# Tiles of split operands made 32 bytes longer

## The chip, the core and the metric

The kernel runs on one core of a Trainium2 chip. The metric is the time of one execution on the device in microseconds (us). Of the kernel before there are three timed runs, 637.49 to 638.16 us with a median of 637.85, and one profiled execution, from which every duration below is taken.

The core's engines work at the same time and wait for each other by semaphores. PE (TensorE) multiplies matrices: a weight load (LDWEIGHTS, shown as PEld) puts the stationary operand into the array, then a matmul streams the moving operand through it. ACT (ScalarE) and DVE (VectorE) work element by element, POOL (GpSimd) does little here, and SP issues DMAs. Tiles lie in the on-chip memory as 128 partitions by so many bytes.

## The reference

A decoder trunk of two layers on 256 positions of width 1024, in float32. Each layer adds a token mixer and then a squared-ReLU channel mixer to the residual `h`, each on a normed input:

```
for i in range(2):
    u = rmsnorm(h, norm_mix[i])
    h = h + (dsw_mixer if i == 0 else moba_mixer)(u, w_qkv, q_gain, k_gain, w_o, rel_bias)
    h = h + square(relu(rmsnorm(h, norm_ffn[i]) @ w1)) @ w2          # 1024 -> 4096 -> 1024
```

The first mixer ("a") is dilated sliding-window attention: 24 heads of 64 in three groups of window and dilation, merged by their softmax denominators. The second ("b") is block-sparse attention with 16 heads; its block has 256 positions, so at this length it is causal attention. Both norm q and k per head and add a relative-position bias. All weights together are some 110 MB, and each is used once.

## The kernel before, in words

**Split operands.** The large products are computed from split float32 numbers. A weight `w` (after its gain) and an activation `u` each become a high part, rounded to the type float32r, and a low part, the rest. `mm3` (L228 to L231) then adds three matmuls in one accumulator in PSUM: high by high (L229), high by low, low by high. The product of the low parts is left out. In the up-projection of the channel mixer the three are written out (L652 to L654).

**The weight stream.** All weights are cut into units of 256 rows by 512 columns, in the order of use (`plan`). SP loads a unit into one of 5 `raw` tiles. ACT makes the high part (`next_hi`, L165 without and L167 with a gain) and DVE the low part (`next_lo`, L175 and L177). They are written into one of 7 `hi` and one of 7 `lo` tiles, each of 128 partitions by 2 by 512 numbers, 4096 bytes a partition. `weight` hands a slice of 128 rows to the matmuls, and `used` gives a unit back. `beat`, called every one or two groups of matmuls, paces the stream: on every second beat it makes one more slice, and it starts whatever was put off by `defer` to this beat. So the order on each engine is written out by the program; no planner reorders it.

**The activations.** `norm_transpose` turns a half of the residual by PE into PSUM, and ACT and DVE split it into the pair `u` (two halves of 4 by 256 numbers, high and low, one buffer each: 4 tiles). `project` multiplies u (stationary, 128 columns) by the weights (moving, 512 columns) for q, k and v. `attend` computes logits, softmax and weighted values with plain float32 matmuls, and its `finish` splits the result into a pair of tiles of the tag `ol`, 4 buffers. `wo_group` multiplies these by the output weights (512 moving columns).

**The channel mixer.** In `ffn`, `up(j)` makes 512 of the 4096 hidden columns: here the weights are stationary (128 columns) and u is moving (256 columns). ReLU, square and split go to a pair `hh`, `hl` of the same tag `ol`. `down(j)` multiplies the pair (stationary) by the second weights (moving, 512 columns) into the accumulators `y`. `up(j + 1)` is issued ahead of `down(j)`, eight times, in each of two layers.

**Where tiles lie.** Pools follow each other in the memory, and the slots of a tag lie one after the other. The tiles that the change touches have a size of 4096 bytes each, a multiple of 128, and start at multiples of 128.

Of the kernel before, what the change touches and what calls it, by code (L numbers as in the profile page):

```python
# [25 lines left out]
F32R = mybir.dt.float32r  # L26
# [4 lines left out]
P = 128  # L31
S = 256
# [15 lines left out]
SPLIT = 7  # L48
# [19 lines left out]
def trunk(ctx, tc, x, rel_bias, norm_mix, norm_ffn, a_w_qkv, a_q_gain, a_k_gain, a_w_o,  # L68
# [4 lines left out]
    wp = ctx.enter_context(tc.tile_pool(name="wp", bufs=1))  # L73
    act = ctx.enter_context(tc.tile_pool(name="act", bufs=1))
# [6 lines left out]
    def bank(tag, name):  # L81
        return ps.tile([P, 512], F32, tag=tag, bufs=2, name=name)

    def work(tag, bufs, name):
        return act.tile([P, 512], F32, tag=tag, bufs=bufs, name=name)

# [43 lines left out]
    raw, split = {}, {}  # L130
# [21 lines left out]
    def parts(s):  # L152
        i, c = divmod(s, 2)
        return raw[i][:, c, :], split[i][0][:, c, :], split[i][1][:, c, :], units[i][1]

    def next_hi():
        i, c = divmod(st["hi"], 2)
        if i >= len(units) or i >= st["first"] + SPLIT:
            return False
        if c == 0:  # L160
            split[i] = (wp.tile([P, 2, 512], F32R, tag="hi", bufs=SPLIT, name=f"hi_{i}"),
                        wp.tile([P, 2, 512], F32R, tag="lo", bufs=SPLIT, name=f"lo_{i}"))
        w, hi, _, gain = parts(st["hi"])
        if gain is None:
            nc.scalar.activation(hi, w, AF.Copy)  # L165
        else:
            nc.scalar.activation(hi, w, AF.Copy, scale=gt[:, gain + c:gain + c + 1])  # L167
        st["hi"] += 1
        return True
# [19 lines left out]
    def weight(key, k):  # L189

        i = index[key, k // 2]
        s = 2 * i + k % 2
        st["asked"] = max(st["asked"], s + 1)
        while st["hi"] <= s:
            assert next_hi(), (key, k)
        while st["lo"] <= s:
            next_lo()
        return split[i][0][:, k % 2, :], split[i][1][:, k % 2, :]

    def used(key, k):  # L200
        done.add(index[key, k // 2])
        while st["first"] in done:
            st["first"] += 1

    def defer(beats, fn):
        st["seq"] += 1
        later.append((st["beat"] + beats, st["seq"], fn))

    def beat(n=1):

        for _ in range(n):
            st["beat"] += 1
            while True:
                due = sorted(e for e in later if e[0] <= st["beat"])
                if not due:
                    break
                later.remove(due[0])
                due[0][2]()
            if st["beat"] % 2 == 0 or st["lo"] < st["asked"] + 4:
                next_slice()  # L220
# [7 lines left out]
    def mm3(acc, a, b, first, last):  # L228
        nc.tensor.matmul(acc, lhsT=a[0], rhs=b[0], start=first, stop=False)  # L229
        nc.tensor.matmul(acc, lhsT=a[0], rhs=b[1], start=False, stop=False)  # L230
        nc.tensor.matmul(acc, lhsT=a[1], rhs=b[0], start=False, stop=last)  # L231


    h = const.tile([P, NT, D], F32, name="h")
# [15 lines left out]
    rel = lead.tile([REL_BUCKETS, NG * HG], F32, name="rel")  # L250
    nc.sync.dma_start(rel, rel_bias)
    idle = work("z", 3, "idle")[:, 0:P]
    nc.vector.memset(idle, 0.0)
    warm_ps = bank("o", "warm_ps")
# [87 lines left out]
    u = {}  # L342
    rstd = {}

    def norm_transpose(which, half, t, natural):

        if t == 0:
            u[half] = tuple(act.tile([P, 4, S], F32R, tag=f"u{half}{s}", bufs=1, name=f"u{s}_{which}_{half}")
                            for s in ("h", "l"))
        tp = bank("tp", f"ut_{which}_{half}_{t}")  # L350
        for c in range(4):
            k = 4 * half + c
            nc.tensor.transpose(out=tp[:, c * P:(c + 1) * P], in_=h[:, t, k * P:(k + 1) * P], identity=ident)
        hi, lo = u[half]
        i = tp.rearrange("p (c q) -> p c q", c=4)
        if natural:
            hi, lo = (z.rearrange("p c (q t) -> p t c q", t=NT)[:, t] for z in (hi, lo))
        else:
            hi, lo = (z[:, :, t * P:(t + 1) * P] for z in (hi, lo))
        nc.scalar.activation(hi, i, AF.Copy)  # L360
        nc.vector.tensor_sub(lo, i, hi.bitcast(F32))
# [40 lines left out]
    def ux(k, cols):  # L402
        hi, lo = u[k // 4]
        return hi[:, k % 4, cols], lo[:, k % 4, cols]


    V, T, oT = {}, {}, {}
# [79 lines left out]
    def attend(layer):  # L487
# [6 lines left out]
        bias, probs, turned, o = {}, {}, {}, {}  # L494
# [90 lines left out]
        def finish(p):  # L585

            if p % 4 == 0:
                oT[p // 4] = tuple(act.tile([P, 4, S], F32R, tag="ol", bufs=4, name=f"o{s}_{layer}_{p}") for s in "hl")
            hi, lo = (z[:, p % 4, :] for z in oT[p // 4])
            i = o[p][:, 0:S]  # L590
            if layer == "b":
                hi, lo = (z.rearrange("p (b t q) -> p t q b", b=2, t=2) for z in (hi, lo))
                i = i.rearrange("p (t q b) -> p t q b", t=2, b=2)
            nc.scalar.activation(hi, i, AF.Copy)
            nc.vector.tensor_sub(lo, i, hi.bitcast(F32))
# [28 lines left out]
    def ffn(i, after):  # L624
        hid, y = {}, {}

        def up(j):
            key = ("up", i, j)
            hh, hl = hid[j] = tuple(act.tile([P, 4, S], F32R, tag="ol", bufs=4, name=f"h{s}_{i}_{j}") for s in "hl")
            first = j == 0  # L630
            banks = {}

            def relu2(b, c0, n):
                w = n * S
                r = work("z", 3, f"r_{i}_{j}_{b}")[:, :w]
                defer(1, lambda: nc.scalar.activation(r, banks[b][:, :w], AF.Relu))  # L636
                ho, lo = (z[:, c0:c0 + n, :].rearrange("p c q -> p (c q)") for z in (hh, hl))
                defer(3, lambda: nc.vector.tensor_mul(r, r, r))  # L638
                defer(5, lambda: nc.scalar.activation(ho, r, AF.Copy))
                defer(7, lambda: nc.vector.tensor_sub(lo, r, ho.bitcast(F32)))  # L640

            for c, ks in [(c, r) for r in (range(4), range(4, 8)) for c in range(4)] if first else \
                    [(c, range(8)) for c in range(4)]:
                b, off = (c, 0) if first else (c // 2, c % 2 * S)
                if b not in banks:
                    banks[b] = bank("acc" if b < 2 else "o", f"up_{i}_{j}_{b}")
                o = banks[b][:, off:off + S]
                for k in ks:
                    whi, wlo = weight(key, k)
                    uh, ul = ux(k, slice(0, S))  # L650
                    cols = slice(c * P, (c + 1) * P)
                    nc.tensor.matmul(o, lhsT=whi[:, cols], rhs=uh, start=k == 0, stop=False)  # L652
                    nc.tensor.matmul(o, lhsT=whi[:, cols], rhs=ul, start=False, stop=False)  # L653
                    nc.tensor.matmul(o, lhsT=wlo[:, cols], rhs=uh, start=False, stop=k == 7)  # L654
                    if c == 3 and k % 2:
                        used(key, k)
                    if k % 2:
                        beat()
                if ks[-1] == 7 and first:
                    relu2(b, c, 1)  # L660
                elif ks[-1] == 7 and c % 2:
                    relu2(b, c - 1, 2)

        def down(j):
            hh, hl = hid[j]
            for n in range(2):
                key = ("down", i, j, n)
                if j == 0:
                    y[n] = [bank("so"[n], f"y_{i}_{n}_{t}") for t in range(NT)]
                tail = i == 1 and j == 7 and n == 1  # L670
                for k, t in [(k, t) for t in range(NT) for k in range(4)] if tail else \
                        [(k, t) for k in range(4) for t in range(NT)]:
                        q = slice(t * P, (t + 1) * P)
                        mm3(y[n][t], (hh[:, k, q], hl[:, k, q]), weight(key, k), j == 0 and k == 0, j == 7 and k == 3)
                        if t == 1 and k % 2:
                            used(key, k)
                        beat()
                if j == 7:
                    after(n, y[n])

        up(0)
        for j in range(8):
            if j < 7:
                up(j + 1)
            down(j)
# [105 lines left out]
```

## Time and profile before

| | |
|---|---|
| median of 3 runs | 637.85 us (637.49 to 638.16) |
| profiled execution | 637.99 us |
| its span, first to last instruction | 636.2 us |
| PE busy | 630.7 us, 3902 matmuls |
| PEld busy | 545.1 us, 3902 weight loads |
| DVE busy | 426.5 us |
| ACT busy | 384.3 us |
| POOL busy | 36.6 us |
| mean granted clock of PE | 0.999 of full speed |
| HBM read | 111.81 MB, 178 GB/s over the span |

The busy time of an engine is the time in which at least one of its instructions ran. Matmuls follow each other before the one ahead has ended, so a busy PE can still be faster or slower, and the distance between the starts of two matmuls says more than the duration of one. Arrows in the rows read "written <- read".

### The profile page before, as it was taken

The numbers are of one execution on the slowest core, as the hardware profiler recorded it, in microseconds if no ns is written. First come the engines' busy times: TensorE is split into PE (matmuls) and PEld (weight loads), VectorE is DVE, ScalarE is ACT, GpSimd is POOL, SyncE is SP. The second block draws the span as 40 slices with busy tenths as digits, with TensorE's granted clock in tenths as the row PEclk, the third lists the DMA queues.
The fourth block names the chain that finished last, engine by engine and source line by source line (L and its number), as shares of the span: only waits on it lengthen the run. The fifth ranks groups of instructions, "written<-read, shape, count | busy, mean of one in ns | idle before, by whom it ended". The sixth has DMA issues, their size and how long they took to land.

```text
span 636.2 us, 10379 instructions
## 1 busy us (share of the span) xinstructions
PE 630.7 (99%) x3902; PEld 545.1 (86%) x3902; DVE 426.5 (67%) x767; ACT 384.3 (60%) x742; POOL 36.6 (6%) x23
## 2 busy tenths in 40 slices
PE   8999999999999999999999999999999999999997
PEld 7778888778989989988988887777998899899886
DVE  5878989846865476467447789886776745754651
ACT  6876876665765365356437868766655644653540
POOL 1222230000000000000000322000000000000000
PEclk9999999999999999999999999999999999999999
DMA  7986566434655674574456566653467446645701
GB/s 247 318 197 229 130 199 173 144 100 123 213 162 185 214 223 132 179 261 137 167 179 201 198 187 188 165 164 122 152 199 261 134 170 229 208 132 192 250 15 67
DMA packets 74538, 113.62 MB, mean 179 GB/s; under 512 B 4584, under 2 KB 30504, under 8 KB 74488
## 3 DMA queue, kind: packets, MB, share of 16 engines
q1 hardware_dynamic: 74312, 112.82, 55.9%
q8 instruction: 31, 0.51, 0.3%
q14 instruction: 19, 0.16, 0.1%
q10 hardware_dynamic: 176, 0.14, 0.1%
HBM read 111.81 MB, written 1.13 MB: 178 GB/s over the span
## 4 chain that ended last, share of the span: by engine, by line
PE 98%; DMA 1%; DVE 0%; SPq 0%; DVEq 0%; issue 0%
PE up L654 10%; PE up L653 10%; PE up L652 10%; PE y L230 9%; PE y L231 9%; PE y L229 9%; PE acc_a L229 6%; PE acc_a L230 5%; PE acc_a L231 5%; PE acc_b L229 4%; PE acc_b L231 3%; PE acc_b L230 3%; PE s_a L518 1%; PE o_a L583 1%; PE wo_b L229 1%; PE wo_b L231 1%
## 5 line engine op out<-in xcount | busy, mean ns | idle before, releaser
L177 DVE SCALAR_TENSOR_TENSOR lo<-raw,gt,hi 128x512 fp32r<-128x512 f32 x248 | 174.7, 746 | 7.2 <-ACT hi L167 7.1
L167 ACT ACTIVATE hi<-raw,gt 128x512 fp32r<-128x512 f32 x248 | 162.9, 712 | 5.7 <-PE y L231 2.8
L652 PE MATMUL up<-uh,hi 128*128 128x256 f32 x512 | 145.1, 283 | 0.0
L654 PE MATMUL up<-uh,lo 128*128 128x256 f32 x512 | 144.9, 283 | 0.0
L653 PE MATMUL up<-ul,hi 128*128 128x256 f32 x512 | 144.9, 283 | 0.0
L175 DVE TENSOR_TENSOR lo<-raw,hi 128x512 fp32r<-128x512 f32 x152 | 98.7, 687 | 44.4 <-ACT hi L165 44.0
L165 ACT ACTIVATE hi<-raw 128x512 fp32r<-128x512 f32 x152 | 88.0, 623 | 54.1 <-PE y L231 28.1
L229 PE MATMUL y<-hi,hh 128*128 128x512 f32 x256 | 99.9, 390 | 0.0
L230 PE MATMUL y<-lo,hh 128*128 128x512 f32 x256 | 99.8, 390 | 0.0
L231 PE MATMUL y<-hi,hl 128*128 128x512 f32 x256 | 99.6, 389 | 0.0
L653 PEld LDWEIGHTS up<-ul,hi 128*128 128x128 f32 x512 | 98.2, 192 | 0.6
L652 PEld LDWEIGHTS up<-uh,hi 128*128 128x128 f32 x512 | 98.2, 192 | 0.5
L654 PEld LDWEIGHTS up<-uh,lo 128*128 128x128 f32 x512 | 98.2, 192 | 0.0
L638 DVE TENSOR_TENSOR r<-r 128x512 f32<-128x512 f32 (+1 forms) x36 | 22.7, 632 | 68.4 <-ACT r L636 68.4
L636 ACT ACTIVATE r<-up 128x512 f32<-128x512 f32 (+1 forms) x36 | 19.8, 550 | 76.1 <-PE up L654 75.7
L229 PE MATMUL acc_a<-hi,uh 128*128 128x512 f32 x144 | 60.6, 421 | 0.0
L230 PE MATMUL acc_a<-lo,uh 128*128 128x512 f32 x144 | 56.8, 395 | 0.0
L231 PE MATMUL acc_a<-hi,ul 128*128 128x512 f32 x144 | 56.8, 394 | 0.0
L231 PEld LDWEIGHTS y<-hi,hl 128*128 128x128 f32 x256 | 48.1, 188 | 10.0
L229 PEld LDWEIGHTS y<-hi,hh 128*128 128x128 f32 x256 | 48.1, 188 | 9.6
L230 PEld LDWEIGHTS y<-lo,hh 128*128 128x128 f32 x256 | 48.1, 188 | 9.5
L229 PE MATMUL acc_b<-hi,uh 128*128 128x512 f32 x96 | 40.2, 419 | 0.0
(128 smaller groups left out, 778.3 us busy)
## 6 DMA issues: line engine op xcount, KB each, us to landing
raw<-in_ffn_w_dram SPq DMA_DIRECT2D x128, 512.0 KB, 4.8
raw<-in_a_w_qkv_dram SPq DMA_DIRECT2D x64, 256.0 KB, 4.2
raw<-in_b_w_qkv_dram SPq DMA_DIRECT2D x24, 512.0 KB, 4.6
raw<-in_b_w_o_dram SPq DMA_DIRECT2D x8, 512.0 KB, 4.8
bias_a<-vdram_a SPq DMA_DIRECT2D x20, 128.0 KB, 5.9
raw<-in_a_w_qkv_dram SPq DMA_DIRECT2D x4, 512.0 KB, 6.5
raw<-in_a_w_o_dram SPq DMA_DIRECT2D x4, 512.0 KB
bias_b<-vdram_b SPq DMA_DIRECT2D x8, 256.0 KB, 4.9
```

Of the source, the lines that this page charges most:

```text
L165: nc.scalar.activation(hi, w, AF.Copy)
L167: nc.scalar.activation(hi, w, AF.Copy, scale=gt[:, gain + c:gain + c + 1])
L175: nc.vector.tensor_sub(lo, w, hi.bitcast(F32))
L177: nc.vector.scalar_tensor_tensor(lo, w, gt[:, gain + c:gain + c + 1], hi.bitcast(F32), op0=ALU.mult, op1=ALU.subtract)
L229: nc.tensor.matmul(acc, lhsT=a[0], rhs=b[0], start=first, stop=False)
L230: nc.tensor.matmul(acc, lhsT=a[0], rhs=b[1], start=False, stop=False)
L231: nc.tensor.matmul(acc, lhsT=a[1], rhs=b[0], start=False, stop=last)
L636: defer(1, lambda: nc.scalar.activation(r, banks[b][:, :w], AF.Relu))
L638: defer(3, lambda: nc.vector.tensor_mul(r, r, r))
L652: nc.tensor.matmul(o, lhsT=whi[:, cols], rhs=uh, start=k == 0, stop=False)
L653: nc.tensor.matmul(o, lhsT=whi[:, cols], rhs=ul, start=False, stop=False)
L654: nc.tensor.matmul(o, lhsT=wlo[:, cols], rhs=uh, start=False, stop=k == 7)
```

## The change

The helper `wide` allocates a tile of 1032 float32r numbers, 4128 bytes a partition, and returns a view on the first 1024 of them in the shape that was asked for. It takes the place of the plain allocation in four places: the tiles `hi` and `lo` of the split weights, the pairs `u`, and the two uses of the tag `ol` (attention output and hidden activations). The last 8 numbers of each tile are never written or read. No instruction's shape or order is edited. The tiles behind those in the memory move by multiples of 32 bytes.

```diff
+    def wide(pool, tag, bufs, name, a):
+
+        z = pool.tile([P, 1032], F32R, tag=tag, bufs=bufs, name=name)
+        return z[:, :1024].rearrange("p (a n) -> p a n", a=a)
...
         if c == 0:
-            split[i] = (wp.tile([P, 2, 512], F32R, tag="hi", bufs=SPLIT, name=f"hi_{i}"),
-                        wp.tile([P, 2, 512], F32R, tag="lo", bufs=SPLIT, name=f"lo_{i}"))
+            split[i] = tuple(wide(wp, part, SPLIT, f"{part}_{i}", 2) for part in ("hi", "lo"))
...
         if t == 0:
-            u[half] = tuple(act.tile([P, 4, S], F32R, tag=f"u{half}{s}", bufs=1, name=f"u{s}_{which}_{half}")
-                            for s in ("h", "l"))
+            u[half] = tuple(wide(act, f"u{half}{s}", 1, f"u{s}_{which}_{half}", 4) for s in "hl")
...
             if p % 4 == 0:
-                oT[p // 4] = tuple(act.tile([P, 4, S], F32R, tag="ol", bufs=4, name=f"o{s}_{layer}_{p}") for s in "hl")
+                oT[p // 4] = tuple(wide(act, "ol", 4, f"o{s}_{layer}_{p}", 4) for s in "hl")
...
-            hh, hl = hid[j] = tuple(act.tile([P, 4, S], F32R, tag="ol", bufs=4, name=f"h{s}_{i}_{j}") for s in "hl")
+            hh, hl = hid[j] = tuple(wide(act, "ol", 4, f"h{s}_{i}_{j}", 4) for s in "hl")
```

## Rows read from the trace of the kernel before

**Rows 1.** The page, busy us (share of the span) and instructions by engine.

```profile
PE 630.7 (99%) x3902; PEld 545.1 (86%) x3902; DVE 426.5 (67%) x767; ACT 384.3 (60%) x742; POOL 36.6 (6%) x23
```

**Rows 2.** The page, the chain of waits that ended last, by engine.

```profile
PE 98%; DMA 1%; DVE 0%; SPq 0%; DVEq 0%; issue 0%
```

**Rows 3.** Groups by line: xcount | busy us, mean ns | idle before; one of three each.

```profile
L652 PE MATMUL up<-uh,hi 128*128 128x256 f32 x512 | 145.1, 283 | 0.0
...
L229 PE MATMUL y<-hi,hh 128*128 128x512 f32 x256 | 99.9, 390 | 0.0
...
L229 PE MATMUL acc_a<-hi,uh 128*128 128x512 f32 x144 | 60.6, 421 | 0.0
...
L229 PE MATMUL acc_b<-hi,uh 128*128 128x512 f32 x96 | 40.2, 419 | 0.0
...
L229 PE MATMUL wo_b<-hi,oh_b 128*128 128x512 f32 x32 | 13.5, 423 | 0.0
...
L229 PE MATMUL wo_a<-hi,oh_a 128*128 128x512 f32 x16 | 7.0, 435 | 0.0
```

**Rows 4.** Timeline of PE, an up stretch: start us, us; first and 27th row.

```profile
235.81 0.28 PE L654 MATMUL up<-uh,lo 128*128 128x256 f32 x1
...
238.93 0.28 PE L653 MATMUL up<-ul,hi 128*128 128x256 f32 x1
```

**Rows 5.** Timeline of PE, a settled down stretch: first and seventh row.

```profile
300.08 0.39 PE L229 MATMUL y<-hi,hh 128*128 128x512 f32 x1
...
301.44 0.39 PE L229 MATMUL y<-hi,hh 128*128 128x512 f32 x1
```

**Rows 6.** Timeline of PE, the first projection: first, fourth, fifth and ninth of nine rows.

```profile
9.15 0.63 PE L231 MATMUL acc_a<-hi,ul 128*128 128x512 f32 x1
...
10.43 0.42 PE L231 MATMUL acc_a<-hi,ul 128*128 128x512 f32 x1
10.69 0.39 PE L229 MATMUL acc_a<-hi,uh 128*128 128x512 f32 x1
...
11.62 0.39 PE L230 MATMUL acc_a<-lo,uh 128*128 128x512 f32 x1
```

**Rows 7.** Timeline of PE, down after up: first and sixth matmul after the switch.

```profile
246.37 0.40 PE L229 MATMUL y<-hi,hh 128*128 128x512 f32 x1
...
247.53 0.39 PE L231 MATMUL y<-hi,hl 128*128 128x512 f32 x1
```

**Rows 8.** Timeline of PEld, the load for the second of these matmuls.

```profile
246.38 0.19 PEld L230 LDWEIGHTS y<-lo,hh 128*128 128x128 f32 x1
```

**Rows 9.** Timeline of PE, projection between logits: first and eighth of eight rows.

```profile
60.16 0.40 PE L231 MATMUL acc_a<-hi,ul 128*128 128x512 f32 x1
...
61.78 0.39 PE L229 MATMUL acc_a<-hi,uh 128*128 128x512 f32 x1
```

**Rows 10.** Groups by line, the splitting of weights on DVE and ACT.

```profile
L177 DVE SCALAR_TENSOR_TENSOR lo<-raw,gt,hi 128x512 fp32r<-128x512 f32 x248 | 174.7, 746 | 7.2 <-ACT hi L167 7.1
L167 ACT ACTIVATE hi<-raw,gt 128x512 fp32r<-128x512 f32 x248 | 162.9, 712 | 5.7 <-PE y L231 2.8 <-DMA raw<-in_a_w_qkv_dram 2.7 <-ACT hi L165 0.2
...
L175 DVE TENSOR_TENSOR lo<-raw,hi 128x512 fp32r<-128x512 f32 x152 | 98.7, 687 | 44.4 <-ACT hi L165 44.0
```

**Rows 11.** Windows: us, busy us (x) of PE, PEld, DVE, ACT, POOL, PEclk, DMA, GB/s.

```profile
330.00:400.00 70.00, 70.00 (x371) 57.02 (x370) 58.27 (x120) 53.64 (x117) 14.21 (x5) 1.00 0.62 188
...
6.00:18.00 12.00, 11.70 (x49) 9.31 (x50) 9.41 (x14) 10.11 (x20) 0.00 (x0) 1.00 0.91 309
```

**Rows 12.** Groups by line, weight loads before which PE waited for a lo.

```profile
L230 PEld LDWEIGHTS acc_a<-lo,uh 128*128 128x128 f32 x144 | 27.4, 190 | 4.8 <-DVE lo L177 0.5
```

**Rows 13.** Groups by line, the splitting of u.

```profile
L361 DVE TENSOR_TENSOR ul<-ut,uh 128x512 fp32r<-128x512 f32 x16 | 11.0, 690 | 10.5 <-ACT uh L360 10.4
...
L360 ACT ACTIVATE uh<-ut 128x512 fp32r<-128x512 f32 x16 | 9.6, 603 | 22.6 <-PE ut L353 22.6
```

**Rows 14.** The chain in order of time, its longest pieces: the first.

```profile
1.19 4.97 DMA h<-in_x_dram
```

## The prediction

> **What bounds the kernel now.** I read the busy times first. TensorE (PE) is busy for 630.7 of the 636.2 us [rows 1]. The chain of waits comes next, and it shows that this is no accident of the average: 98% of the chain that ended last is PE, and of the other engines only a DMA reaches 1% [rows 2]. So the time is the sum of the distances from one matmul's start to the next, and whatever is not in that sum has to be larger than its cover before it counts.
>
> The groups by line give the number of matmuls [rows 3]; the reader takes the counts there, and not the busy times, since those overlap (283 ns for a matmul that follows its neighbour after 120). Up-projection (three lines of 512) has 1536 matmuls with 256 moving columns. The others with split operands have 512 moving columns and come three lines each: y 768, acc_a 432, acc_b 288, wo_b 96, wo_a 48, together 1632. Every one of these 3168 reads a stationary and a moving operand from tiles that the change touches.
>
> The timeline gives the distance. In an up stretch the first row and the 27th start 3.12 us apart: 3.12 / 26 = 120.0 ns [rows 4]. In a settled down stretch six distances take 1.36 us: 226.7 ns [rows 5]. At 2.4 columns per ns, 256 and 512 columns are 106.7 and 213.3 ns, so that each of the matmuls has 13.3 ns over its columns, the same at both lengths. At the start the four rows show something else [rows 6]: three distances from 9.15 to 10.43 us, 427 ns each, which is 512 columns at 1.2 GHz, the lower of the clock's two levels, with nothing over (the clock's row on the page shows no lower level there; the distances do); from 10.69 us on four distances average 232 ns.
>
> The sum: 1536 x 120.0 = 184.3 us and 1632 x 226.7 = 370.0 us, 554.3 of the span of 636.2. The remaining 81.9 us are transposes, logits, the small matmuls, what lies around them and the two ends. What the change can reach on PE is the 13.3 ns: 3168 x 13.3 ns = 42.1 us.
>
> **The change part by part.** It adds no instruction, removes none, and moves none: every activation, subtraction, matmul and DMA has the same shape and order. It makes 22 slots longer by 32 bytes a partition (14 of hi and lo, 4 of u, 4 of the tag ol), 704 bytes together. Before, each of these tiles is 4096 bytes, a multiple of 128; after, 4128, so that the start of a slot moves through 0, 32, 64 and 96 modulo 128. A 128-column slice is 512 bytes and keeps its tile's offset. Three costs can follow.
>
> *PE's two reads.* While one matmul's moving operand streams, the next matmul's weights are loaded. In the trace the load starts at 246.38 us, with the matmul that started at 246.37 [rows 7, 8]. If both reads used one of four 32-byte places in turn and blocked each other where they met, 13.3 ns would be the price, and other offsets would change it. The bounds of that: of four offsets three differ from before, so up to 3/4 x 42.1 = 31.6 us could go (606.4 us from the profiled 637.99), and as much could come if the offset of today is the good one (669.6 us). The value I take is 0, for two reasons. First, the offset is not held: in up stretches one load of 128 columns (512 bytes) goes with 256 moving columns (1024 bytes), so the moving read runs 512 bytes, four times 128, ahead of the load in each matmul; in 512-column matmuls it is 1536 bytes, twelve times 128. At steady rates the two reads meet at each offset equally often wherever they start, and a shift of the start by 32 bytes changes which meeting is first, not how many there are. Secondly, 13.3 ns is the same for two lengths and for pairs of quite different tiles, which fits a fixed price of a weight change better.
>
> What speaks for a sensitivity is that the 512-column distance is not always 226.7. After a switch from up to y five distances average 232 ns [rows 7], and in the projection between transposes seven average 231.4 [rows 9]. They come at the same places of the pattern and settle, so they follow the spacing of loads and matmuls; a read that is sensitive to that by a few ns may be sensitive to 32 bytes too. The nearest row to a cost is therefore 5 ns on a 512-column matmul, 1632 x 5.0 = 8.2 us at most.
>
> The Trainium skill bears on this place ("TensorE: Matmul & The Clock Gate", section "Part 2: What happens when you issue a matmul"): it says that PE reads the moving operand and the weights through two independent ports, and that a load takes nothing from the running matmul. By that rule the padding is worth 0. The same page (section "Wait — 56ns, not 53.3ns?") has a matmul cost its columns plus about 2.5 ns at full clock; by an estimate from it, 3168 matmuls would lie 34 us lower than the rows show. The trace's 13.3 ns disagrees with the second statement, and this is why I don't hold the first for settled: by rule 637.9 us, by the row's remainder, were three quarters of it contention, about 612 us.
>
> *ScalarE and VectorE.* ACT writes hi, DVE reads raw and hi and writes lo; raw stays at 0 modulo 128, hi and lo shift. The costliest are 248 subtractions at 746 ns and 248 activations at 712 ns [rows 10]. I take 0. The bounds are from the rows: DVE's two-input forms lie between 687 and 746 ns, so I allow 59 ns either way for 400 subtractions, 23.6 us of DVE work. All of it lies beside PE: in the tightest long stretch DVE is busy 58.3 of 70 us and has 11.7 left, while about 70/636 of 23.6 us, 2.6 us, would be added [rows 11]. A gain there is worth nothing, as PE has waited for a lo only once, 0.5 us [rows 12]. Only at the start is there little cover: from 6 to 18 us ACT is busy 10.1 of 12 us. With 10% more there, up to 1 us would show.
>
> *Order and DMAs.* The tile is now one row of 1032 with a view on it. If dependencies were drawn more coarsely for the view, the place is u: its two writers per half each take every other 128 columns of four chunks, so that ranges of the two interleave. That would be a wait of ACT for DVE's 16 subtractions of 690 ns [rows 13], 11.0 us if all of them stood in PE's way, and 0 as I take it, since both halves of a tile are written before the matmuls that need them. Tiles behind the padded ones (z, q and k turned, bias, h) also move by multiples of 32 bytes. Of these h and bias are written by DMA; landings are slack except x at the start, where the chain has 4.97 us of it [rows 14]; a tenth of that either way is 0.5 us.
>
> Sum: 0 + 0 + 0. The profiled execution took 637.99 us (its span of 636.2 and 1.8 around it); the median of the three runs is 637.85, 0.14 lower. I forecast 637.8 us, no change. What counts as one is 0.2%, 1.3 us: about what a measurement of this kernel can tell.
>
> **The rivals.** *Faster: the reads of PE collide less.* For it: 13.3 ns at the full pace and nothing over at half the pace [rows 4 to 6] is how two reads that compete for one memory would look. Against it: the sweep through all offsets, and the equal price at both lengths. If one pair in four falls on a better offset, 42.1 / 4 = 10.5 us go: 627.3 us. *Slower: the settled rhythm is lost.* Its place is the 512-column matmuls, above all y, which now settle at 226.7. Where a pair's offset differs from before (three in four of 1632), the distance stays at the 231.7 ns of the unsettled stretches: 1224 x 5.0 = 6.1 us, 644.0 us. It decides as soon as the distance depends on more than about 1.3 us / 1632 = 0.8 ns per matmul. For it: rows 7 and 9; against it: unsettled distances follow a switch of shape or a transpose, and the addresses don't change there. *Slower: new waits for u.* 11.0 us exposed at most; half of it gives 643.4 us. Against it: same-engine writers need no wait. *The padding does nothing*, since slots are rounded up and stay 128 apart: 637.85 us, not to be told from my forecast by time, but by distances equal in every stretch.
>
> **How the numbers follow.** No change 0.58 (of this 0.03 that slots don't shift); faster by PE's reads 0.25; slower by a lost rhythm 0.12, by waits 0.05. Of the faster case I give 0.16 to sizes up to 10.5 us and 0.09 beyond; of the slower ones 0.13 up to 7 us and 0.04 beyond. A range from 627 to 645 us holds 0.58 + 0.16 + 0.13 = 0.87; drawn in further, it would end at prices that have a row behind them, and it stays open to 0.13 at the two ends of the bounds (606 and 670). The likeliest case's own range is 636.6 to 639.1.
>
> **What would show it.** Right: up distances of 120.0 ns and settled y distances of 226.7 ns in all stretches, whichever slots are in use, PE about 630.7 us busy, and chain as before; DVE's 746 and ACT's 712 ns within 10 ns. If PE's reads matter, distances differ from slot to slot in a cycle of the seven hi and lo slots, and the up stretches tell it at once, as 0.1 ns of all 1536 would be 0.15 us. Wrong in the DVE step: longer subtractions and PE idle before a lo. Wrong in the order step: idle of PE before the first matmuls after a norm. The forecast falls if the up or the y distance moves by more than 0.8 ns on average.

## The result, and the profile after

The changed kernel takes 641.61 us (median of 4 runs, 641.47 to 642.05), the kernel before, in 4 runs beside it, 637.87 (637.49 to 638.16). The ratio is 1.0060, 95% interval 1.0044 to 1.0076: slower by 3.7 us, or 0.6%. The forecast was no change.

The page of the changed kernel, busy times and the chain by engine, answers to [rows 1, 2]:

```profile
PE 633.6 (99%) x3902; PEld 542.8 (85%) x3902; DVE 426.4 (67%) x767; ACT 384.7 (60%) x742; POOL 36.6 (6%) x23
...
PE 98%; DMA 1%; DVE 0%; SPq 0%; ACT 0%; DVEq 0%; issue 0%; ACTq 0%
```

PE is still the whole chain, with as many instructions, and is busy 2.9 us longer; the span grew from 636.2 to 640.3 us. The other engines did not change. The costliest groups by line of the changed kernel, beside [rows 10, 13]:

```profile
L181 DVE SCALAR_TENSOR_TENSOR lo<-raw,gt,hi 128x512 fp32r<-128x512 f32 x248 | 174.6, 745 | 7.5 <-ACT hi L171 7.3
L171 ACT ACTIVATE hi<-raw,gt 128x512 fp32r<-128x512 f32 x248 | 163.0, 713 | 5.8 <-DMA raw<-in_a_w_qkv_dram 2.6
L179 DVE TENSOR_TENSOR lo<-raw,hi 128x512 fp32r<-128x512 f32 x152 | 98.6, 686 | 46.6 <-ACT hi L169 46.3
...
L364 DVE TENSOR_TENSOR ul<-ut,uh 128x512 fp32r<-128x512 f32 x16 | 11.0, 690 | 11.0 <-ACT uh L363 11.0
```

Each duration is within 1 ns of before. So the time lies in the distances between matmuls, and the timeline shows it. PE in the changed kernel, a stretch of y and the stretch of up behind it, first and last row of each:

```profile
230.43 0.40 PE L233 MATMUL y<-hi,hh 128*128 128x512 f32 x1
...
235.30 0.40 PE L233 MATMUL y<-hi,hh 128*128 128x512 f32 x1
...
239.17 0.28 PE L655 MATMUL up<-uh,hi 128*128 128x256 f32 x1
...
242.38 0.28 PE L655 MATMUL up<-uh,hi 128*128 128x256 f32 x1
```

y: 21 distances in 4.87 us, 231.9 ns, where settled stretches had 226.7 [rows 5]. Up: 27 distances in 3.21 us, 118.9 ns, where there were 120.0 [rows 4]. Neither settles any more: single distances of y lie between 224 and 240 ns, of up between 112 and 129. The windows of the changed kernel show the same as a count:

```profile
6.00:18.00 12.00, 10.77 (x45) 8.58 (x46) 9.29 (x14) 9.80 (x19) 0.00 (x0) 0.86 0.89 301
330.00:400.00 70.00, 70.00 (x367) 56.47 (x366) 55.75 (x113) 50.65 (x106) 14.21 (x5) 1.00 0.57 179
```

In the 70 us from 330, PE is busy throughout as before, but starts 367 matmuls where it started 371 [rows 11], at the full clock in both. In the first window the granted clock is 0.86 where it was 1.00.

All kernels here issue the same 3902 matmuls in the same order. Paired one by one, the differences of the distances, each put to the matmul that it begins with, give this in us against the trace of before, for the changed kernel (first line) and for the experiments below:

| kernel | up | y | acc_a, acc_b, wo | rest | sum |
|---|---|---|---|---|---|
| the change | -2.13 | +3.60 | +2.61 | -0.03 | +4.05 |
| e1 weights only | -2.64 | +3.26 | +1.96 | -0.05 | +2.53 |
| e2 activations only | -2.18 | +4.16 | +2.43 | -0.03 | +4.38 |
| e3 gap of 32 | -4.93 | +4.67 | +3.58 | -0.11 | +3.21 |
| e4 gap of 64 | -3.31 | +4.73 | +3.38 | -0.09 | +4.71 |
| e5 u at 32 | -3.21 | -0.04 | +1.69 | -0.13 | -1.69 |
| e6 hidden at 32 | -0.03 | +4.62 | -0.12 | -0.08 | +4.39 |
| e7 longer, not shifted | -0.01 | +3.09 | +0.33 | -0.14 | +3.27 |
| e8 map, slots +128 | -2.40 | +3.56 | +1.29 | -0.11 | +2.34 |
| e9 map, slots +256 | -3.28 | +3.65 | -0.29 | +0.04 | +0.12 |
| e10 map, slots +256 | -1.58 | +3.06 | +1.17 | -0.02 | +2.63 |
| e11 u at 32, slots +256 | -4.92 | -0.04 | +1.33 | +0.44 | -3.19 |
| e12 weights at 64 and 192 | -9.65 | -0.02 | -0.40 | +0.02 | -10.05 |
| e13 u at 192 and 64 | -3.99 | -0.34 | +0.90 | +0.06 | -3.37 |

Of the changed kernel's 4.05 us, 0.66 had come by the 40th matmul, at the start. PE there, in the changed kernel:

```profile
9.59 0.63 PE L233 MATMUL acc_a<-hi,uh 128*128 128x512 f32 x1
...
11.30 0.63 PE L234 MATMUL acc_a<-lo,uh 128*128 128x512 f32 x1
11.73 0.48 PE L235 MATMUL acc_a<-hi,ul 128*128 128x512 f32 x1
12.04 0.40 PE L233 MATMUL acc_a<-hi,uh 128*128 128x512 f32 x1
```

Five distances from 9.59 to 11.73 us are some 427 ns each, the lower clock level; before, the full level was there some 1.3 us earlier [rows 6]. The kernel before has such executions too: of nine runs in the series beside e1 to e4, four at a mean granted clock of 0.997 took 638.33 to 638.70 us, and five at 0.999 to 1.000 took 637.78 to 638.05 (the mean clock doesn't tell all: beside e11 one at 1.000 took 639.70). The profiled run of the changed kernel is at 0.997, so about 0.5 us of the trace's 4.05 is put down to that execution; the medians differ by 3.74. In e10, e11 and e13 the start is later in the same way: 1.17, 1.79 and 1.02 us by the 40th matmul, which is as much as their whole column for acc and wo, or more.

### The profile page after: what moved, and what is told of

It is laid out like the page before. It is cut to its first block, busy times and chain, and to the rows that moved or that the text cites. A ratio compares the mean times of both kernels' runs of the same rounds, so it can differ in the third digit from the quotient of the medians.

```text
span 640.3 us, 10379 instructions
## 1 busy us (share of the span) xinstructions
PE 633.6 (99%) x3902; PEld 542.8 (85%) x3902; DVE 426.4 (67%) x767; ACT 384.7 (60%) x742; POOL 36.6 (6%) x23
## 4 chain that ended last, share of the span: by engine, by line
PE 98%; DMA 1%; DVE 0%; SPq 0%; ACT 0%; DVEq 0%; issue 0%; ACTq 0%
PE up L656 10%; PE up L655 9%; PE up L657 9%; PE y L235 9%; PE y L234 9%; PE y L233 9%; PE acc_a L233 6%; PE acc_a L234 5%; PE acc_a L235 5%; PE acc_b L233 4%; PE acc_b L235 3%; PE acc_b L234 3%; PE s_a L521 1%; PE o_a L586 1%; PE wo_b L233 1%; PE wo_b L234 1%
## 5 line engine op out<-in xcount | busy, mean ns | idle before, releaser
L235 PE MATMUL y<-hi,hl 128*128 128x512 f32 x256 | 101.0, 395 | 0.0
L234 PE MATMUL y<-lo,hh 128*128 128x512 f32 x256 | 100.8, 394 | 0.0
L233 PE MATMUL y<-hi,hh 128*128 128x512 f32 x256 | 100.8, 394 | 0.0
L655 PEld LDWEIGHTS up<-uh,hi 128*128 128x128 f32 x512 | 96.5, 188 | 0.6
L656 PEld LDWEIGHTS up<-ul,hi 128*128 128x128 f32 x512 | 96.5, 188 | 0.6
L657 PEld LDWEIGHTS up<-uh,lo 128*128 128x128 f32 x512 | 96.6, 189 | 0.0
L233 PE MATMUL acc_a<-hi,uh 128*128 128x512 f32 x144 | 60.9, 423 | 0.6 <-ACT hi L171 0.6
L234 PE MATMUL acc_a<-lo,uh 128*128 128x512 f32 x144 | 57.5, 400 | 0.3 <-DVE lo L181 0.3
L235 PEld LDWEIGHTS y<-hi,hl 128*128 128x128 f32 x256 | 48.1, 188 | 11.1
L235 PE MATMUL acc_a<-hi,ul 128*128 128x512 f32 x144 | 57.3, 398 | 0.0
L234 PEld LDWEIGHTS y<-lo,hh 128*128 128x128 f32 x256 | 48.1, 188 | 10.8
L233 PEld LDWEIGHTS y<-hi,hh 128*128 128x128 f32 x256 | 48.1, 188 | 10.6
L233 PE MATMUL acc_b<-hi,uh 128*128 128x512 f32 x96 | 40.4, 420 | 0.0
```

## The experiments

A place is a tile's start in bytes modulo the period in question, counted from where the kernel before has that tile; so in the kernel before all these tiles are at 0. "y at 64 64" means that hh starts at 64 and hl at 64. A distance is always from one matmul's start to the next one's.

**Which tiles.** *e1* lengthens hi and lo alone, *e2* the activations u and ol alone.

```diff
 # e1
+            split[i] = tuple(wide(wp, part, SPLIT, f"{part}_{i}", 2) for part in ("hi", "lo"))
 # e2
+            u[half] = tuple(wide(act, f"u{half}{s}", 1, f"u{s}_{which}_{half}", 4) for s in "hl")
...
+                oT[p // 4] = tuple(wide(act, "ol", 4, f"o{s}_{layer}_{p}", 4) for s in "hl")
...
+            hh, hl = hid[j] = tuple(wide(act, "ol", 4, f"h{s}_{i}_{j}", 4) for s in "hl")
```

> Only hi and lo are 32 bytes longer; u and the tag ol keep 4096 bytes and all lie at 64 modulo 128. Theory A (the distance of two matmuls depends on where in 128 bytes the moving read and the next weight load lie to each other; equal offsets from pair to pair let the rhythm settle, changing ones do not): the weights' offset changes with every slot and between hi and lo, so the 512-column distance is 230 to 233 ns and the up distance 118 to 119.5, time 640 to 642 us. Theory B (each pair of offsets has its own fixed price, no matter what came before): about the same here, 640 to 642. Theory C (the start, where the full clock came 1.3 us later, and other tiles' places make the difference): distances as before, 637.5 to 638.5.

> Only u and the tag ol are 32 bytes longer; hi and lo stay at 0 modulo 128. Theory A: in y the stationary operand alternates between hh and hl, 32 bytes apart, in a fixed order of three, so the rhythm can settle but elsewhere: 512-column distances between 226 and 233, up 118 to 120, time 636 to 641 us. Theory B: pairs with unlike offsets cost about 232 to 234 against 227 with like ones, so y rises by 4 to 5 ns, time 640 to 642. Theory C: 637.5 to 638.5.

e1 took 640.61 us against 638.05 (ratio 1.0043, 1.0030 to 1.0055), e2 642.85 against 638.05 (1.0070, 1.0058 to 1.0083). Each half alone costs, and the two sums of the table (2.53 and 4.38) do not add up to the whole (4.05). So the price is not a sum over tiles; this fits one that belongs to pairs of tiles.

**Length or place.** *e3* and *e4* leave all tiles as they were and put one unused tile ahead of the activations, of 32 and of 64 bytes, so that every activation is shifted by the same amount against the weights.

```diff
 # e3; e4 has 16 in place of 8
+    act.tile([P, 8], F32, tag="gap", bufs=1, name="gap")
```

> No tile is longer; one unused tile of 32 bytes ahead of the activations moves all of them to 32 modulo 128, while all weights stay at 0. So moving and stationary operand of every split matmul lie 32 bytes apart, always. Theory A: the rhythm settles as before (one distance per stage, spread under 1 ns), possibly at another value; the long unsettled stretches of the changed kernel don't appear; time 632 to 641. Theory B (unlike offsets cost 5 ns more in 512-column matmuls, about 1.3 ns less in up): distances 232 to 234 and 118 to 119, time 642 to 645. Theory C: 637.5 to 638.5.

> As the one with a gap of 32 bytes, with 64: all activations at 64 modulo 128, all weights at 0. Theory A: settled distances, one value per stage; if the places repeat every 64 bytes, exactly those of before (226.7 and 120.0, 637.85 us), otherwise another value within 632 to 641. Theory B: 232 to 234 and 118 to 119, 642 to 645. Theory C: 637.5 to 638.5.

e3: 640.96 against 638.05 (1.0043, 1.0031 to 1.0056). e4: 642.67 (1.0074, 1.0060 to 1.0088). No tile is longer here and no slot moves against its neighbours, and yet most of the loss is there. PE in e3, up after the switch:

```profile
303.91 0.28 PE L653 MATMUL up<-uh,hi 128*128 128x256 f32 x1
...
304.96 0.28 PE L653 MATMUL up<-uh,hi 128*128 128x256 f32 x1
```

Nine distances in 1.05 us: 116.7 ns, where there were 120.0. The mean stays the same from block to block, while single distances repeat a pattern between 113 and 120 ns. The 512-column matmuls, y among them, have 233.3 instead of 226.7 in the same way. In e4 up has 117.8 and the 512-column ones 233.3 to 234. So one fixed shift makes up faster and y slower: the place of the activation against the weight changes the distance, for each shape otherwise.

**One use at a time.** *e5* shifts u by 32 bytes in the two up-projections alone, *e6* the hidden pair alone. *e7* is the control of e6: as long, but not shifted. The tiles are 4224 bytes, a multiple of 128.

```diff
+    def at(pool, tag, bufs, name, a, skip=0):
+        z = pool.tile([P, 1056], F32R, tag=tag, bufs=bufs, name=name)
+        return z[:, skip:skip + 1024].rearrange("p (a n) -> p a n", a=a)
 # e5
+            u[half] = tuple(at(act, f"u{half}{s}", 1, f"u{s}_{which}_{half}", 4, 8 * (which % 2)) for s in "hl")
 # e6; e7 has 0 in place of 8
+            hh, hl = hid[j] = tuple(at(act, "ol", 4, f"h{s}_{i}_{j}", 4, 8) for s in "hl")
```

> Only u of the channel mixer's norms starts 32 bytes into its tile (u of the projections, hidden tiles and weights stay at 0 modulo 128; the four u tiles are 128 bytes longer to make room). So only the up matmuls have unlike offsets. Theory A (what counts is where the moving read and the next weight load lie to each other, and the sign depends on the length: with 32 bytes apart up settles lower, 512 columns higher): up distance 116.5 to 117.5 ns, y and the projections as before, 1536 x about 3 ns less, 632.5 to 634.5 us, faster than the kernel before by 0.6 to 0.9%. Rival D (the weights' own order, or tiles of other engines, made up faster in the run with the gap): up stays at 120.0, 637.5 to 638.5.

> Only the hidden pairs hh and hl start 32 bytes into their tiles (128 bytes longer each); the attention output, u and the weights stay at 0 modulo 128. So only y, 768 of 1632 matmuls with 512 columns, has unlike offsets. Theory A: y settles at 233 to 234 ns and costs 4.5 to 5 us, everything else as before: 642 to 643.5 us. Rival D: y stays at 227, 637.5 to 638.5.

> The tiles of the tag ol are 128 bytes longer and the data starts at their first byte, so that every tile of the kernel keeps its place modulo 128. Theory A: distances and time as before, 637.5 to 638.5 us. Rival E (the length or the strided view costs, by waits or otherwise, and not the place): y or the whole is slower by 0.3% or more, 640 or above.

All three stand against 638.3 us. e6 took 643.07 (1.0073, 1.0059 to 1.0087): up 120.0 as before, y 233.3, as expected. PE in e6, a stretch of y, 12 distances in 2.80 us:

```profile
295.83 0.40 PE L233 MATMUL y<-hi,hh 128*128 128x512 f32 x1
...
298.63 0.40 PE L233 MATMUL y<-hi,hh 128*128 128x512 f32 x1
```

e5 took 636.74 (0.9973, 0.9962 to 0.9985), with up at 117.4 to 118.4 and y at 227; it misses its expectation by some 2 to 4 us, and so does e7, which should have shown nothing and took 641.06 (1.0041, 1.0028 to 1.0055). PE in e7, a stretch of y:

```profile
296.42 0.39 PE L233 MATMUL y<-hi,hh 128*128 128x512 f32 x1
296.64 0.40 PE L234 MATMUL y<-lo,hh 128*128 128x512 f32 x1
296.88 0.40 PE L235 MATMUL y<-hi,hl 128*128 128x512 f32 x1
297.11 0.39 PE L233 MATMUL y<-hi,hh 128*128 128x512 f32 x1
297.34 0.40 PE L234 MATMUL y<-lo,hh 128*128 128x512 f32 x1
297.57 0.40 PE L235 MATMUL y<-hi,hl 128*128 128x512 f32 x1
297.81 0.39 PE L233 MATMUL y<-hi,hh 128*128 128x512 f32 x1
298.03 0.40 PE L234 MATMUL y<-lo,hh 128*128 128x512 f32 x1
```

The reader is to take the distances by step: from L233 to L234 it is 0.22 or 0.23 us, from L234 to L235 0.23 or 0.24, from L235 to L233 0.23 or 0.24. Over the whole kernel the three are 227, 232.5 and 234 ns. The tiles' places modulo 128 are those of before, so the period is not 128. With slots of 4224 bytes a neighbour lies 128 apart modulo 256, and hh and hl are neighbours: modulo 256, y is at 0 128 in e7 and at 32 160 in e6. The same holds for uh and ul in e5, whose acc steps are 227, 233 and 234. There e5 lost a part of its expected gain (+1.69 us in the table), and another in up, which with u at 32 and 160 gained 3.21 us where 5 were expected.

**Maps.** Three kernels give each of the eight blocks j of the two channel mixers places of its own. *e8*, laid out before the above was read, uses slots of 4224 bytes; *e9* and *e10* use slots of 4352, a multiple of 256. In all of them one or two buffers of the turned probabilities were given up for the space, here and in e11 to e13 (NPT); the matmuls that use them moved by 0.02 us at most.

```diff
 # e8, floats by mixer and block: weights of up units and hidden pairs
+SKIP = ((0, 4, 8, 12, 16, 20, 24, 28), (0, 1, 2, 3, 5, 6, 7, 10))
 # e9, bytes: u by norm (high, low), hidden pairs by mixer and block
+UP = ((0, 0), (64, 192), (0, 0), (32, 160))
+DOWN = (((0, 0), (64, 64), (128, 128), (192, 192), (0, 64), (0, 128), (0, 192), (64, 192)),
+        ((192, 64), (32, 32), (96, 96), (160, 160), (224, 224), (16, 16), (8, 8), (4, 4)))
 # e10
+UP = ((0, 0), (64, 0), (0, 0), (128, 128))
+DOWN = (((0, 0), (12, 12), (24, 24), (28, 28), (40, 40), (48, 48), (56, 56), (80, 80)),
+        ((112, 112), (144, 144), (176, 176), (208, 208), (240, 240), (252, 252), (0, 16), (16, 0)))
```

> A look at many offsets in one run: in the first layer's channel mixer the weights of up(j) and the hidden pair of j start at 0, 16, 32, 48, 64, 80, 96, 112 bytes for j = 0 to 7, in the second at 0, 4, 8, 12, 20, 24, 28, 40; u and the down weights stay at 0 modulo 128; pT has 11 buffers and not 12, to make room. The distances of each j are read from the trace. Theory A: each j settles at its own value; 0 gives 120.0 and 226.7, 32 and 96 about 117 and 233, 64 about 118 and 233.5. If the places come in pieces of 32 bytes, 4 to 28 bytes give the values of 0; if the two reads are sensitive to single steps of a column, they lie between. Theory B (a fixed price by pair of places) expects the same values without settling at a change of j. The whole time tells nothing.

> u and the tag ol are 256 bytes longer, so that slots differ by multiples of 256 bytes; weights are untouched. What counts after the run with tiles longer by 128 (y slower by 3 us, at the steps where the weight load changes between hh and hl) is the place modulo 256, if theory A holds with that period: projections and wo keep 227 ns. Rival E (length) would slow them as it did y. Hidden pairs (high, low) start at 0 0, 64 64, 128 128, 192 192, 0 64, 0 128, 0 192, 64 192 bytes in the first channel mixer and 192 64, 32 32, 96 96, 160 160, 224 224, 16 16, 8 8, 4 4 in the second: theory A expects 226.7 at 0 0 only, 232 to 234 at most others. u of the up matmuls starts at 64 and 192 (high, low) in the first mixer and 32 and 160 in the second: the run before had one stretch at 113.5 ns with 64 bytes between weights and u, so 113 to 114 or 117 to 118 in the first, 116 to 119 in the second. pT has 11 buffers and not 12.

> The same with other places. Hidden pairs at 0 0, 12 12, 24 24, 28 28, 40 40, 48 48, 56 56, 80 80 bytes in the first mixer and 112 112, 144 144, 176 176, 208 208, 240 240, 252 252, 0 16, 16 0 in the second; u of the up matmuls at 64 and 0 (high, low) in the first and 128 and 128 in the second. Theory A: projections and wo keep 227 ns, y 226.7 at 0 0 only, steps of a few columns already leave it; up settles at its own value in each mixer, between 113 and 120. Theory B: values by pair of places, the same wherever the pair stands.

One run each. e8: 640.43 us against 638.3; its y blocks lie unsettled between 230 and 233, and it separated little, but the up block with weights at 64 bytes ran at 113.4 ns after its first dozen matmuls, others at 117 to 120. e9: 638.11 against 637.84; e10: 640.61. In e9 acc (229) and wo (229 to 231, waits left out) are as in the kernel before, and y at 0 0 is 226.7 there and in e10, though the tiles are 256 bytes longer. So length by itself costs nothing, and 256 apart counts as the same place. By place of the hidden pair, y in ns:

| y at | ns | y at | ns |
|---|---|---|---|
| 0 0 | 226.7 | 64 64 | 233.3 |
| 8 8 | 230.7 | 96 96 | 234.3 |
| 12 12 | 233.3 | 112 112 | 233.3 |
| 16 16 | 233.3 | 128 128 | 232.4 |
| 24 24 | 231.2 | 176 176 | 229.8 |
| 32 32 | 233.3 | 192 192 | 229.0 |
| 48 48 | 233.3 | 208 208 | 231.8 |
| 56 56 | 233.3 | 240 240 | 226.7 |

Also 28, 40, 144, 160, 224 and 252 give 233.3 to 233.4, 4 4 gives 232.5, and the mixed pairs 0 64, 0 128 and 0 192 give 230.9 to 231.2. 0 0 and 240 240 are the pairs at one place that reach 226.7, and the kernel before had the first of them. Like places are not needed for it: the mixed pairs 0 16 and 16 0 reach 226.7 too, while 16 16 has 233.3. PE in e10, a stretch of y at 0 16, 18 distances in 4.08 us:

```profile
619.87 0.39 PE L236 MATMUL y<-hi,hh 128*128 128x512 f32 x1
...
623.95 0.39 PE L236 MATMUL y<-hi,hh 128*128 128x512 f32 x1
```

For up no place of u in these two runs came near the 113.4 of e8: 117.0 to 120.0 ns.

**A version for the period of 256.** *e11* is e5 with slots of 4352 bytes. *e12* leaves all activations where they were and starts the weights of up units at 64 (hi) and 192 (lo). *e13* shifts u instead, so that in the first mixer the weights loaded during a matmul lie as far from the u that streams meanwhile as in e12.

```diff
 # at() as above with tiles of 1088 numbers and skip in bytes; e11
+UP = ((0, 0), (32, 32), (0, 0), (32, 32))
 # e12
+UP = ((64, 192), (64, 192))
+            where = [UP[k[0][1]] for k, v in index.items() if v == i and k[0][0] == "up"]
+            split[i] = tuple(at(wp, part, SPLIT, f"{part}_{i}", 2, (where + [(0, 0)])[0][n])
+                             for n, part in enumerate(("hi", "lo")))
 # e13
+UP = ((0, 0), (192, 64), (0, 0), (192, 192))
```

> The four u tiles are 256 bytes longer (pT has 11 buffers and not 12) and u of the channel mixer starts 32 bytes into them; weights, hidden tiles and u of the projections keep their places modulo 256. Theory A with a period of 256 bytes: up 116.7 ns as in the run with a gap of 32, and now without what that run and the one with 128-byte steps lost elsewhere: projections, wo and y at the distances of before, so 1536 x 3.3 = 5 us less, 632.3 to 634.0 us, 0.6 to 0.9% faster than before. Rival E (length, or the period is 128 and the losses came from elsewhere): projections at 232, 636 to 637.5.

> Weight tiles are 256 bytes longer (pT has 10 buffers); in units of the up matmuls hi starts at 64 and lo at 192 bytes, in all other units at 0; u and hidden tiles are as before. This is the pattern of the one stretch that ran at 113.5 ns. If a rhythm once reached is kept and the pattern leads to it: up 113.3 to 114, 1536 x 6.5 = 10 us less, 627 to 629 us. If that stretch was an accident of what came before it: up 117 to 118.5, 633.5 to 636. Theory B, prices by pair of places: the value of the earlier stretch for these pairs, 113.5, from the first matmul on. Rival E: 640 or more.

> Does only the place of the next weight load relative to the moving operand count? u of the first channel mixer starts at 192 (high) and 64 (low) bytes, weights at 0: relative to each other as in the run with weights at 64 and 192, by way of the other operand. In the second mixer u starts at 192 for both. If only that difference counts and the rhythm is found: 113 to 114 in the first; if the weights' own changes of place count too: 116 to 119. In the second a settled value between 113 and 118.

e11 took 633.30 against 637.81 (0.9927, 0.9913 to 0.9941), as expected with the period of 256: up 116.7 in all blocks, y 226.7, acc and wo, past the start, as before. The profiled run is the longest of its six (634.89 us), with the late start given above. PE in e11, 24 distances in 2.81 us:

```profile
236.84 0.28 PE L657 MATMUL up<-uh,hi 128*128 128x256 f32 x1
...
239.65 0.28 PE L657 MATMUL up<-uh,hi 128*128 128x256 f32 x1
```

e12 took 628.19 against 637.81 (0.9853, 0.9838 to 0.9869). It beats the kernel before by 9.6 us and the changed kernel, measured in the first series, by 13.4. The page of e12, and PE in it, up behind a block of y and later y:

```profile
PE 619.0 (99%) x3902; PEld 533.6 (85%) x3902; DVE 426.3 (68%) x767; ACT 383.9 (61%) x742; POOL 36.6 (6%) x23
```

```profile
232.18 0.28 PE L658 MATMUL up<-uh,hi 128*128 128x256 f32 x1
...
232.88 0.28 PE L658 MATMUL up<-uh,hi 128*128 128x256 f32 x1
...
233.90 0.28 PE L658 MATMUL up<-uh,hi 128*128 128x256 f32 x1
...
296.24 0.39 PE L235 MATMUL y<-hi,hh 128*128 128x512 f32 x1
...
296.92 0.39 PE L235 MATMUL y<-hi,hh 128*128 128x512 f32 x1
```

The first six distances take 0.70 us (117 ns), the next nine 1.02 (113.3); y has three in 0.68 (226.7). The whole gain is in up, 9.65 of 10.05 us.

e13, one run, took 634.61. In its first mixer up has 117.8 ns, not 113.3, so the difference between the two places that PE reads does not decide alone. Its second mixer has the same places (192 192) in every block. PE in e13, an up stretch before the first block of y and one after it:

```profile
468.14 0.28 PE L657 MATMUL up<-uh,hi 128*128 128x256 f32 x1
...
470.52 0.28 PE L657 MATMUL up<-uh,hi 128*128 128x256 f32 x1
...
488.35 0.28 PE L657 MATMUL up<-uh,hi 128*128 128x256 f32 x1
...
490.82 0.28 PE L657 MATMUL up<-uh,hi 128*128 128x256 f32 x1
```

21 distances take 2.38 us in the first (113.3 ns) and 2.47 in the second (117.6; 117.8 over all blocks behind the first y). The same places run in two rhythms, so a fixed price by pair of places, the rival to a rhythm that places and history set, can't be the whole account.

## Why the prediction was wrong

**The bound** was read rightly. PE's distances are the time: the table's columns add up to the span's growth (640.3 less 636.2), and e12's 10.05 us in the table came back as 9.6 between the medians. In the sum of before, 226.7 ns was some 2 ns low for acc and wo, which lie at 229 to 231 in that trace with waits left out; the difference, some 2 us, belongs to them and not to the remaining 81.9 us.

**PE's two reads**, valued at 0, is the step that failed. It had two reasons. The sweep argument, that the moving read passes all offsets against the load, so that a shift of the start changes nothing, is refuted by e3: one shift of 32 bytes, the same for all, moves up from 120.0 to 116.7 ns and y from 226.7 to 233.3. It also counted modulo 128, and e7 with e9 shows 256. The second reason, an equal 13.3 ns over the columns at both lengths as a sign of a fixed price, was a coincidence of the place 0: with other places up has 6.7 to 13.3 ns over its columns and y 13.3 to 20 and more. What stands in its place: the distance of two matmuls with split operands depends on the places modulo 256 of what they read and load (e3, e7, e11, e12), and on the rhythm in which PE already runs (e13). Before the change all tiles lay at 0, among the best places found for 512 columns and the poorest for 256; no stretch settled at a lower y or a higher up. The change spreads the tiles over eight places modulo 256 (4128 is 32 more than a multiple of it), the pairs change, and no rhythm settles: y at 231.9 and up at 118.9 ns in the rows above. How much of this is the price of the new pairs and how much the lost rhythm, no run separates.

The Trainium skill ("TensorE: Matmul & The Clock Gate", section "Part 2: What happens when you issue a matmul") has two independent ports for moving data and weights; by its rule, too, the change was worth 0. Measured, the same instructions lie 113.3 to 120.0 and 226.7 to 234.3 ns apart by the places of their tiles. Whether it is the load that holds the stream up, no run here shows.

**The rivals.** "The settled rhythm is lost" was the right one, with a chance of 0.12. It took 5.0 ns for three in four of the 512-column matmuls; y gave 3.60 us / 768 = 4.7 ns over all of its matmuls. Against its 6.1 us, y and the acc and wo lines gave 3.60 + 2.61 = 6.21 in the trace, of which some 0.5 is the later clock. What it lacked is the gain in up, 2.13 us (1.4 ns by 1536), which brings its 644.0 down to 641.9, beside the measured 641.6. The faster rival named the right kind of cause, with the wrong sign for this layout. That its 10.5 us are near the 9.6 that e12 got by choosing places is chance: it took one pair in four and the whole 13.3 ns, and e12 took 6.3 ns off each up matmul (9.65 us / 1536) and next to nothing off the others. Waits for u did not come (DVE's idle before ul is 11.0 us where it was 10.5, beside PE), and slots do move.

**ScalarE and VectorE, order and DMAs** were right at 0: 745, 713 and 686 ns in the rows above, the same chain, and a sum of -0.03 us over all matmuls that the change doesn't touch (shifts of some 0.5 us cancel at the start, and past it no group of them moved by more than 0.04).

The range of 627 to 645 us held the time; the chance of slower, 0.17, was too small, since the row that spoke for a sensitivity, 13.3 ns over the columns at the full clock and nothing at the lower one, was set aside for an argument that no row had tested.

## What to carry to other kernels

Where PE is the whole chain, compare the distance of its matmuls, by shape, with their columns, and try the places of the operands' tiles before an argument that places can't matter: here two start offsets for one kind of tile, in slots 256 bytes longer and with no instruction more, were worth 1.5%. A place belongs to a pair and a shape: give each use its own (here weights of up at 64 and 192, all others at 0 modulo 256), and keep slots a multiple of 256 long, so that a place stays. Whether these places carry to other shapes or types is not tested. A layout that looks spread, as this one, mixes good places with bad ones and settles at neither.

## What the runs showed of the hardware

- Split matmuls settle at distances between 113.3 and 120.0 ns for 256 columns (116.7 and 117.8 among them) and between 226.7 and 234.3 for 512, which is 6.7 to 21 ns over the columns. The most frequent two for 512, 226.7 and 233.3, lie 6.7 ns apart, as do the ends for 256: 16 columns' time at 2.4 per ns. 116.7 is a distance of its own in e11, where settled single distances are 116 or 117 ns; in e3 the same mean is a repeated pattern between 113 and 120.
- The place counts modulo 256 bytes, with steps as small as 8 bytes telling (226.7, 230.7 and 233.3 ns at 0 0, 8 8 and 12 12).
- There is a memory in it: the same places at 113.3 before and 117.6 after a block of y (e13). Behind the up stretches of e13 y is at 226.7 at once, where the kernel before has some 229 for a dozen matmuls, though y's places are the same.
- At the lower clock level 512 columns take 427 ns at the start of both kernels, nothing over the columns, though their places differ.
- Open: what in PE or in the memory makes the price (that two reads collide is inferred from the dependence on pairs and from its absence at the lower level, not shown), why e12 reaches 113.3 ns where e13 with the same differences does not, and what decides when the clock rises at the start.
